# A hybrid attention and Fourier kernel: in its second mixer the products with the values follow the scores by two units instead of three, and query tiles are loaded one unit earlier

## The chip, the cores and the metric

The kernel runs on one core of a Trainium2 chip. The metric is device time in microseconds (us) of one execution, and lower is better. Three executions of the kernel before took 1214.49, 1209.16 and 1210.06 us, with a median of 1210.06 us. All times below the whole come from one more execution, the profiled one, which took 1214.27 us.

Engines are named as in the profile: PE is TensorE with PEld as its loading of weights, DVE is VectorE, ACT is ScalarE, POOL is GpSimd, and SP is the engine that issues the DMAs.

## The reference, cut to what matters

A step of a diffusion backbone has two layers over 1024 latent tokens and 256 context tokens, 1280 rows of 1024 channels. The even layer has two attention mixers: A is global, B looks at a window of 128 tokens on either side and at the context, with a learned "sink" logit per head. Each has 8 query heads and 2 key heads of 64 channels. The gated outputs of both are concatenated and projected. The odd layer is a Fourier mixer.

```python
oa = dense_block_attention(qa, ka ++ ka_ctx, va ++ va_ctx)      # mixer A: 1280 keys
ob = window_attention_with_ctx(qb, kb, vb, kb_ctx, vb_ctx, sink) # mixer B: up to 384 + 256 keys
y  = concatenate([oa * silu(ga), ob * silu(gb)], axis=-1) @ w_out
x  = x + gate * y
# odd layer
u, gate = split(h @ w_in);  y = (real(fft2(u)) * silu(gate)) @ w_out
```

All of it is float32. The kernel splits a float32 number into a high and a low part and forms a product as three matmuls, high by high, high by low and low by high (`mm3`, L256, whose matmuls have line L263).

## The kernel before

**Units.** The 1280 rows are 10 blocks of 128 rows. A unit of attention, written t_gp below, is a block t, a group g of four query heads (g 0 and 1 belong to mixer A, 2 and 3 to mixer B) and a pair p of those heads. So 6_30 is block 6, group 3, first pair. `attend` (L1077) goes through all 40 units of mixer A, and then through the 40 of mixer B in the order of blocks 0, 2, 3, 4, 7, 6, 5, 1, 8, 9 (`ORD_B`, L27), in which group 3 of a block comes four tiles behind its group 2.

**What a unit does.** `soft` (L932) forms the scores on PE (sL and sC at L924, in mixer B sC at L924 and the band sB at L996). DVE moves them out of PSUM and keeps the extreme of each row (`keep`, L958; in mixer B the mask at L1002). ACT then takes the exponential (L965) into a buffer of zone "p". `weigh` (L1031) transposes this buffer on PE, up to four squares to a PSUM bank (L1041), and ACT and DVE split each bank into a high and a low half of one buffer of zone "pt" (L275 and L1044). PE multiplies these by the values (tile av, L1047), and the result goes out to DRAM (tensor od, stored at L1064). Behind the second pair of group 3 `totals` (L1012) transposes the sums of the exponentials (tile tt, L1023) and stores them (tensor scd, L1028).

**The lag.** `attend` appends each unit's scores to a list, and runs `weigh` for the oldest while the list is longer than the lag: 1 unit in mixer A (`LAG_A`), 3 in mixer B (`LAG_B`). Zone "p" has 4 buffers. In mixer B a unit holds one of them.

**Query tiles.** The queries of a block and group are projected, transposed and split in `q_pair`, and written to DRAM (tensor qd). The tile that receives the split, qe, takes the zone in `QE_Z` ("pt", "q", "w", "u", "p") whose free buffer has been free for the longest. `load_q` (L926) reads a tile back by two DMAs of 64 partitions into one of the two buffers of zone "q". `attend` calls it for the next block and group behind the scores of a unit whose pair equals `QPRE` (L1087), which was 1, the second pair.

**Filler.** After each unit PE gets other work from a queue (`Filler`, L90): the projections of queries, keys and gates (ga, stored as tensor gd at L833 to L835), pieces that fold two weight matrices into one (wa, L557), and at the end the output projections. A step r of these is one block of 128 rows in the order 0, 4, 2, 6, 3, 7, 1, 5, 8, 9 (`PAIRS`, L61). Its load, `proj_in` (L1206), reads od, gd and scd, multiplies gate by sums (L1216) and that by od (L1217), and splits the result by ACT (L275) and DVE or POOL (L281). Its `proj_step` (L1315) runs 24 matmuls for each half of the columns, tiles oz{r}0 and oz{r}1 (so oz31 is the second half of step 3), and DVE scales each half (L1238) and adds it (L1239). A load is put into the queue ahead of the step before it.

**Buffers and order.** ZONES (L23) lists the buffers: 26 of "u", 8 of "w", 2 of "q", 3 of "pt", 4 of "p". Step 7's split lies in a "pt" and a "p" buffer, which become free only as the last units end. The program order above is input to a list scheduler (the tile context, L1947), which decides the order on each engine. Each engine then runs its own list in order, so that an instruction that waits holds up all behind it.

Of the kernel before, what the change touches and what calls it, by code (L numbers as in the profile page):

```python
# [22 lines left out]
ZONES = {"u": (26, 1032), "w": (8, 1032), "q": (2, 1024), "pt": (3, 1024), "p": (4, 1280), "h": (9, 512), "e": (4, 256)}  # L23
BIG = ("w", "q", "pt", "p", "u")
UV = ("u",)
FILL_A, FILL_B, LAG_A, LAG_B = 4.4, 2.9, 1, 3
E_PH, E_OH, E_OL, E_WO = "a", "a", "dp", "a"  # L27
EARLY, SPAN = 1, 2
WSTEP = ((2, 1, 2), (1, 0, 1))
# [9 lines left out]
E_ML = ("dp", "dp", "d")  # L39
E_MF, E_MH, LC0 = "da", "d", "ppd"  # L40
EF = 2
QPRE, HOLD = 1, 0
PLACE = (
    ((0, 0, 128),), ((128, 0, 128),), ((385, 0, 127), (256, 127, 1)), ((257, 0, 128),), ((769, 1, 127), (512, 0, 1)),
    ((896, 0, 128),), ((641, 0, 128),), ((513, 0, 128),), ((1024, 0, 128),), ((1153, 0, 127), (1152, 127, 1)),
# [94 lines left out]
def hybrid_step(ctx: ExitStack, tc: tile.TileContext, I, O):  # L140
# [15 lines left out]
    def take(tag, shape, dt=F32):  # L156
        tags = (tag,) if isinstance(tag, str) else tag
        z = min((t for t in tags if spare[t]), key=lambda t: spare[t][0])
        i = spare[z].popleft()[1]
        size = 2 if dt == BF16 else 4  # L160
        for s in shape[1:]:
            size *= s
        assert size <= 4 * ZONES[z][1]
        made[0] += 1
        return Buf(z, i, up.tile(list(shape), dt, tag=f"{z}{i}", name=f"{z}{made[0]}", bufs=1))
# [118 lines left out]
    def load_w(src, width=256, tags="w", gap=None, lc=E_WL, each=None, later=None):  # L284
        out = []
        for kp in range(2):
            hi = take(tags, (P, 4, width), F32R)
            lo = take(tags, (P, 4, width), F32R)
            for j in range(2):
                r0 = (kp * 4 + j * 2) * P  # L290
                if width <= 256:
                    raw = take("h", (P, 2, width))
                else:
                    raw = take(("p", "pt", "q", "w"), (P, 2, width))
                if gap is None:
                    sp.dma_start(raw.a, src[r0 : r0 + 2 * P, :].rearrange("(j p) f -> p j f", p=P))
                else:
                    gap(raw, r0)
                if each is not None:
                    each(raw, kp * 4 + 2 * j)  # L300

                def fin(raw=raw, hi=hi[:, 2 * j : 2 * j + 2, :], lo=lo[:, 2 * j : 2 * j + 2, :]):
                    split(hi, lo, raw.a, XE["wh"], lc)
                    drop(raw)

                if later is None:
                    fin()
                else:
                    later.append(fin)
            out.append((hi, lo))  # L310
        return out
# [239 lines left out]
    def fold_piece(g, kb2, wu, first=False):  # L551
        f = fold["f"]
        acc = bank("t" if first else "g", f"wa{g}{kb2}")
        for i in range(2):
            c0 = (2 * kb2 + i) * P
            for j in range(2):
                pe.matmul(  # L557
                    acc[:, i * 256 : i * 256 + 256], wu[j][:, c0 : c0 + P], f[:, j, :], start=j == 0, stop=j == 1
                )
        if first:  # L560
            if kb2 % 2 == 0:
                early[g, kb2 // 2] = take("u", (P, 4, 256))
            wo = early[g, kb2 // 2][:, 2 * (kb2 % 2) : 2 * (kb2 % 2) + 2, :]
        else:
            wb = take("h", (P, 2, 256))
            wo = wb.a
        copy("wo", "a", wo, acc.rearrange("p (i f) -> p i f", i=2))
        if not first:
            fold_put(g, kb2 * 256, wo)
            drop(wb)  # L570
        if kb2 == 3:
            drop(*wu)
            fold["n"] = fold.get("n", 0) + 1
            if fold["n"] in (EF, 4):
                drop(f)
                del fold["f"]
# [263 lines left out]
    fl_ = Filler()  # L840
# [343 lines left out]
    OB, late = [("u", "w")], [False]  # L1184
# [21 lines left out]
    def proj_in(src, gate, r, resid):  # L1206
        if gate is not None:
            flush_held()
            ol = take(OB[0], (P, 8, P))
            sp.dma_start(ol.a, src[r])  # L1210
            gl = take(OB[0], (P, 8, P))
            rl = take(OB[0], (P, 8, P))
            sp.dma_start(gl.a, gate[r])
            for h in range(2):
                sp.dma_start(rl[64 * h : 64 * h + 64], scd[r, h].partition_broadcast(64))
            pick("pm", XE["pm"]).tensor_mul(gl.a, gl.a, rl.a)  # L1216
            pick("pm", XE["pm"]).tensor_mul(ol.a, ol.a, gl.a)  # L1217
            drop(gl, rl)
        hi, lo = take(OB[0], (P, 8, P), F32R), take(OB[0], (P, 8, P), F32R)
        if gate is not None:  # L1220
            split(hi.a, lo.a, ol.a, E_OH, E_OL)
            drop(ol)
        else:
            for c in range(2):
                split(hi[:, 4 * c : 4 * c + 4, :], lo[:, 4 * c : 4 * c + 4, :], src(c, r), "a", "d")
        xr = take(OB[0], (P, D))
        sp.dma_start(xr.a, resid[r * P : (r + 1) * P, :])
        return hi, lo, xr
# [77 lines left out]
    def proj_load(i, j):  # L1306
        r = pairs[i][j]
        v = r // 8
        if v not in gt0:
            gt0[v] = take(OB[0], (P, D))  # L1310
            sp.dma_start(gt0[v].a, gtd[0, v].partition_broadcast(P))
        ins[r] = proj_in(od, gd, r, I["xp"])
        return 0
# [65 lines left out]
    def can_run(i, j):  # L1379
        r = pairs[i][j]  # L1380

        def fn():
            if sum(len(spare[z]) for z in OB[0]) < NSP or i > EARLY:
                return False
            return all(finished.get(t, 99) + SPAN < clock[0] for t in USES[r])
        return fn

    wgs = []
    steps = [(i, j) for i in range(5) for j in range(2)]

    def late_fold(nm):
        def fn():
            ws[nm] = fold_load(int(nm[1]))
            return 0
        return fn

    for n, nm in enumerate(FLATE.split()):
        fl_.add(0.0, late_fold(nm))
        if n == 0:
            fl_.add(0.0, lambda: proj_load(0, 0), ready=can_run(0, 0))  # L1400
        for k in range(4):
            fl_.add(FC, lambda k=k, nm=nm: fold_piece(int(nm[1]), k, ws[nm]))
    if not FLATE:
        fl_.add(0.0, lambda: proj_load(0, 0), ready=can_run(0, 0))
    for n, ij in enumerate(steps):
        if n == 8:
            fl_.add(0.0, lambda: wgs.append(load_w(I["w_g1"][:, 0:256], tags=BIG)) or 0)
        if n < 9:
            fl_.add(0.0, lambda ij=steps[n + 1]: proj_load(*ij), ready=can_run(*steps[n + 1]))
        fl_.add(7.7, lambda ij=ij: proj_step(*ij))  # L1410

    units = [(t, g, pr) for g in range(2) for t in range(NT) for pr in range(2)]
# [542 lines left out]
```

## Time and profile before

| What | Value |
|---|---|
| median of three runs | 1210.06 us (1209.16 to 1214.49) |
| profiled execution, its own time | 1214.27 us |
| span of its instructions | 1212.4 us |
| granted clock of TensorE, mean over the span | 0.985 of full speed |
| mixer A's units | about 137 to 520 us |
| mixer B's units | about 520 to 820 us |

The page gives busy time by engine and 40 slices of the span, each 30.3 us wide, in which a digit is the busy share in tenths. The time outside the span is 1.9 us. Where PE is idle, the views of waits and of the timeline tell what it waited for, and the view of windows gives busy time, granted clock and DMA share of any stretch.

### The profile page before, as it was taken

How to read it: one execution, taken by the hardware profiler on the slowest of the kernel's cores; microseconds unless marked ns; L12 is line 12 of the kernel's file. 1: busy time of each engine (PE TensorE's matmuls, PEld its weight loads, DVE VectorE, ACT ScalarE, POOL GpSimd, SP SyncE). 2: the span in 40 equal slices, each digit the busy share in tenths (PEclk: the TensorE clock that was granted, in tenths of full speed). 3: DMA queues.
4: the chain of work that ended last, by engine and by line, in shares of the span. 5: the costliest groups of instructions: out<-in, count | busy, mean ns of one | idle time of the engine just before them, and what ended most of it. 6: DMA issues, size and time to landing. Idle time of an engine off the chain costs nothing. (4 is left out here: it accounts for less than half of the span.)

```text
span 1212.4 us, 22083 instructions
## 1 busy us (share of the span) xinstructions
PE 1166.8 (96%) x8103; PEld 1041.6 (86%) x8103; DVE 839.6 (69%) x2000; ACT 576.6 (48%) x1159; POOL 320.1 (26%) x278
## 2 busy tenths in 40 slices
PE   7999999999999999999999999989999999999997
PEld 5787899999999998999888887868877888997886
DVE  3479788877777777678787776878756953367543
ACT  3343466555655555556566675533364224342211
POOL 2255634512332130011010114213202217245001
PEclk9899999999999999999999999989999999999999
DMA  9957412323523233344253686677214435264321
GB/s 317 360 190 260 150 59 66 103 79 108 149 64 101 60 92 113 95 120 121 74 140 81 181 256 198 181 201 219 96 44 136 152 114 169 94 200 151 121 103 53
DMA packets 129840, 168.81 MB, mean 139 GB/s; under 512 B 26298, under 2 KB 86454, under 8 KB 129732
## 3 DMA queue, kind: packets, MB, share of 16 engines
q1 hardware_dynamic: 129732, 167.40, 45.5%
q8 instruction: 64, 1.05, 0.4%
q14 instruction: 44, 0.36, 0.1%
HBM read 123.19 MB, written 44.16 MB: 138 GB/s over the span
## 5 line engine op out<-in xcount | busy, mean ns | idle before, releaser
L1044 DVE TENSOR_TENSOR pt<-pt,pt 128x512 fp32r<-128x512 f32 (+1 forms) x264 | 170.8, 658 | 50.9 <-ACT pt L275 50.1
L275 ACT ACTIVATE pt<-pt 128x512 fp32r<-128x512 f32 (+1 forms) x264 | 146.1, 575 | 83.9 <-PE pt L1041 49.0
L1047 PE MATMUL av<-pt,u 128*128 128x256 f32 x1008 | 167.3, 290 | 1.1 <-DVE e L1058 1.0
L1041 PE MATMUL pt<-identr,p 128*128 128x128 f32 x1008 | 153.7, 273 | 1.5 <-DVE pt L1044 1.5
L1047 PEld LDWEIGHTS av<-pt,u 128*128 128x128 f32 x1008 | 140.1, 190 | 6.2 <-DVE e L1058 2.0
L263 PE MATMUL q<-w,u 128*128 128x256 f32 x960 | 143.4, 287 | 0.2 <-ACT h L725 0.2
L263 PEld LDWEIGHTS q<-w,u 128*128 128x128 f32 x960 | 126.0, 189 | 5.1 <-issue 0.8
L1041 PEld LDWEIGHTS pt<-identr,p 128*128 128x128 f32 x1008 | 118.7, 141 | 7.0 <-issue 1.8
L263 PE MATMUL ga<-u,w 128*128 128x512 f32 (+1 forms) x576 | 124.2, 360 | 0.3 <-DVE h L817 0.2
L965 ACT ACTIVATE p<-p,nm 128x1280 f32<-128x1280 f32 (+1 forms) x80 | 95.3, 1192 | 53.4 <-DVE p L958 52.9
L263 PEld LDWEIGHTS ga<-u,w 128*128 128x128 f32 x576 | 93.6, 188 | 15.1 <-ACT pt L275 0.4
L281 POOL TENSOR_TENSOR w<-h,w 128x512 fp32r<-128x512 f32 x38 | 50.1, 1334 | 130.9 <-DVE w L277 100.4
L924 PE MATMUL sL<-u,q 128*128 128x512 f32 x256 | 82.4, 409 | 1.6 <-DMA q<-qd 1.6
L281 POOL TENSOR_TENSOR u<-h,u 128x512 fp32r<-128x512 f32 x24 | 33.8, 1416 | 158.7 <-ACT u L275 151.8
L965 ACT ACTIVATE p<-p,NM 128x640 f32<-128x640 f32 (+2 forms) x80 | 59.1, 739 | 24.5 <-DVE p L958 24.3
L924 PE MATMUL sC<-u,q 128*128 128x256 f32 x320 | 63.4, 297 | 4.0 <-DVE p L1002 2.0
L263 PE MATMUL oz<-u,u 128*128 128x512 f32 x208 | 60.8, 397 | 2.9 <-DVE h L1238 2.9
L263 PE MATMUL oz<-u,w 128*128 128x512 f32 x192 | 58.3, 396 | 0.0
L958 DVE TENSOR_SCALAR_CACHE_REDUCE p<-sL 128x512 f32<-128x512 f32 x64 | 43.8, 685 | 20.1 <-PE sL L924 15.3
L924 PEld LDWEIGHTS sC<-u,q 128*128 128x128 f32 x320 | 49.5, 190 | 7.7 <-DVE p L1002 2.6
L698 POOL TENSOR_TENSOR h<-h,rope 128x512 f32<-128x512 f32 (+1 forms) x18 | 21.2, 1180 | 128.2 <-ACT h L781 82.3
L958 DVE TENSOR_SCALAR_CACHE_REDUCE p<-sL,nm 128x512 f32<-128x512 f32 x64 | 47.6, 744 | 8.3 <-PE sL L924 7.0
(721 smaller groups left out, 2584.3 us busy)
## 6 DMA issues: line engine op xcount, KB each, us to landing
q<-qd SPq DMA_DIRECT2D x80, 256.0 KB
h<-i_w_in SPq DMA_DIRECT2D x40, 256.0 KB
p<-i_ada_w SPq DMA_DIRECT2D x18, 512.0 KB
qd<-q SPq DMA_DIRECT2D x36, 256.0 KB
h<-i_w_out SPq DMA_DIRECT2D x32, 256.0 KB
pt<-i_ada_w SPq DMA_DIRECT2D x15, 512.0 KB
q<-i_ada_w SPq DMA_DIRECT2D x11, 512.0 KB
u<-g1d SPq DMA_DIRECT2D x9, 512.0 KB
```

Source lines behind the costliest of these rows:

```text
L263: pe.matmul(out, a, b, start=i == 0, stop=i == n - 1)
L275: act.activation(out, in_, AF.Copy)
L281: pick("lo" + lc, lc).tensor_sub(dst_l, src, dst_h)
L698: pick("rope", XE["rope"]).tensor_mul(t1.rearrange("p t h (b c) -> p t (h b) c", b=2), y.rearrange("p t h (b c) -> p t (h b) c", b=2), cb)
L924: pe.matmul(ps, q_at(q, s, hc), keys, start=s == 0, stop=s == 1)
L958: dve.tensor_scalar(p[i][:, end[i] : end[i] + n], ps, sign, last[i], op0=ALU.mult, op1=ALU.min, accum_out=c)
L965: act.activation(p[i][:, 0 : end[i]], p[i][:, 0 : end[i]], AF.Exp, bias=last[i], scale=-1.0, accum_out=SU[:, t, hd + i, 0:1],)
L1041: pe.transpose(tp[:, jj * 256 + i * P : jj * 256 + i * P + P], p[i][:, off : off + P], ident)
L1044: dve.tensor_sub(pt[:, 1, 0:n], tp[:, 0:n], pt[:, 0, 0:n])
L1047: pe.matmul(acc, vv, pt[:, s, jj * 256 : jj * 256 + 256], start=c + jj + s == 0, stop=c + jj == nt - 1 and s == 1,)
```

## The change

`LAG_B` becomes 2. `QPRE` becomes 0: the next query tile is loaded behind the first pair of a tile, not the second, in both mixers. The loads of the projections go through `load_to`, which with `AHEAD` at 1 issues the same load at the same place as before.

```diff
-FILL_A, FILL_B, LAG_A, LAG_B = 4.4, 2.9, 1, 3
+FILL_A, FILL_B, LAG_A, LAG_B = 4.4, 2.9, 1, 2
-QPRE, HOLD = 1, 0
+QPRE, HOLD, AHEAD = 0, 0, 1
...
+    loaded = [0]
+
+    def load_to(n):
+        while loaded[0] <= min(n, 9):
+            proj_load(*steps[loaded[0]])
+            loaded[0] += 1
+        return 0
...
-            fl_.add(0.0, lambda: proj_load(0, 0), ready=can_run(0, 0))
+            fl_.add(0.0, lambda: load_to(0), ready=can_run(0, 0))
...
-            fl_.add(0.0, lambda ij=steps[n + 1]: proj_load(*ij), ready=can_run(*steps[n + 1]))
+            fl_.add(0.0, lambda n=n: load_to(n + (AHEAD if late[0] else 1)), ready=can_run(*steps[n + 1]))
```

Since the scheduler orders the whole program, rows move on every engine. Three places are shown. In a row the numbers behind a name are the program's own and differ between the two kernels.

On SP, around the query tile of block 6, group 3, before. The first and the last row are the two halves of the tile (q926); between them stand stores of attention outputs (od), of sums (scd) and of gates (gd), two loads of step 0 (u919, u920) and a store of fold work (wd); the line of dots leaves out two stores of od and one of scd.

```order
L929 DMA q926_9263<-qd_69 64x2x512
...
L1028 DMA scd_77<-e882_8972 16x1
L833 DMA gd_73<-h909_9203 128x128
L834 DMA gd_73<-h909_9203 128x127
L835 DMA gd_73<-h909_9203 128x1
L1213 DMA u919_9230<-gd_73 128x1024
L1064 DMA od_72<-e881_8959 64x2x127
L1064 DMA od_72<-e881_8959 64x2x1
L1215 DMA u920_9231<-scd_77 64x1024 x2
L547 DMA wd_74<-h924_9248 128x2x256
L929 DMA q926_9263<-qd_69 64x2x512
```

The same place now; the tile is q908.

```order
L929 DMA q908_9176<-qd_69 64x2x512
L1064 DMA od_72<-e858_8781 64x2x127
L1064 DMA od_72<-e858_8781 64x2x1
L1028 DMA scd_77<-e875_8907 16x127
L1028 DMA scd_77<-e875_8907 16x1
L833 DMA gd_73<-h890_9045 128x128
L834 DMA gd_73<-h890_9045 128x127
L835 DMA gd_73<-h890_9045 128x1
L1064 DMA od_72<-e874_8894 64x2x127
L1064 DMA od_72<-e874_8894 64x2x1
L929 DMA q908_9176<-qd_69 64x2x512
```

The second half stands 10 rows behind the first, not 13, and the loads of step 0 (u919, u920) and the store wd are no longer ahead of it.

On PE, between the second pair's scores of block 6, group 3 and the first transposes of its first pair (pt6_300), before.

```order
L996 MATMUL sB6_310_9416<-u682_7065,q926_9263 128x384 x2
L996 MATMUL sB6_311_9421<-u682_7065,q926_9263 128x384 x2
L924 MATMUL sC6_31_9409<-u684_7067,q926_9263 128x256 x2
L1041 MATMUL pt8_210_9480<-identr_85,p925_9253 128x128 x4
L1047 MATMUL av7_31_9347<-pt937_9353,u684_7067 128x256 x4
L1047 MATMUL av7_31_9347<-pt938_9365,u683_7066 128x256 x4
L557 MATMUL wa31_9398<-h914_9219,w934_9319 128x256
L557 MATMUL wa31_9398<-h914_9219,w935_9320 128x256
L557 MATMUL wa31_9398<-h914_9219,w934_9319 128x256
L557 MATMUL wa31_9398<-h914_9219,w935_9320 128x256
L1041 MATMUL pt6_300_9513<-identr_85,p936_9325 128x128
```

Now, with the last score row of 6_30 as the first row here.

```order
L924 MATMUL sC6_30_9371<-u683_7045,q908_9176 128x256 x2
L924 MATMUL sC6_31_9431<-u683_7045,q908_9176 128x256 x2
L1041 MATMUL pt8_200_9396<-identr_85,p907_9166 128x128 x4
...
L996 MATMUL sB6_310_9438<-u681_7043,q908_9176 128x384 x2
L996 MATMUL sB6_311_9443<-u681_7043,q908_9176 128x384 x2
L924 MATMUL sC6_31_9431<-u683_7045,q908_9176 128x256 x2
L1041 MATMUL pt8_210_9452<-identr_85,p930_9287 128x128 x4
L1047 MATMUL av7_31_9297<-pt931_9303,u683_7045 128x256 x4
L1047 MATMUL av7_31_9297<-pt932_9315,u682_7044 128x256 x4
L1041 MATMUL pt6_300_9501<-identr_85,p941_9370 128x128
```

The fold piece that stood right ahead of pt6_300 is gone from there (four rows of another piece, wa21, stand in the place of the line of dots), and so are the value products of 7_30 and the transposed sums tt7, which before stood between the last sC6_30 and the scores of 6_31.

On PE, the end of mixer B, before: the last rows of the second half of step 3, the value products of 9_30, and the start of step 7.

```order
L1047 MATMUL av8_31_10228<-pt1039_10234,u684_7067 128x256 x4
L1023 MATMUL tt9_10306<-identr_85,byp9_10304 16x128
L263 MATMUL oz61_10355<-u911_9210,u1008_9955 128x512
L263 MATMUL oz61_10355<-u910_9209,u1009_9956 128x512
L263 MATMUL oz31_10463<-u816_8428,w1053_10321 128x512
...
L263 MATMUL oz31_10463<-u910_9209,u1054_10322 128x512
L1047 MATMUL av9_30_10260<-pt1043_10266,u684_7067 128x256 x4
L263 MATMUL oz70_10509<-u816_8428,pt1066_10427 128x512
```

Now.

```order
L1047 MATMUL av8_31_10229<-pt1039_10235,u683_7045 128x256 x4
L263 MATMUL oz31_10463<-u822_8470,w1053_10321 128x512
L263 MATMUL oz31_10463<-u823_8471,w1053_10321 128x512
L1023 MATMUL tt9_10306<-identr_85,byp9_10304 16x128
...
L263 MATMUL oz60_10327<-u916_9243,u1014_10006 128x512
L263 MATMUL oz60_10327<-u915_9242,u1015_10007 128x512
L263 MATMUL oz31_10463<-u916_9243,w1053_10321 128x512
L263 MATMUL oz31_10463<-u915_9242,u1054_10322 128x512
L1047 MATMUL av9_31_10279<-pt1046_10285,u683_7045 128x256 x4
L263 MATMUL oz71_10537<-u822_8470,pt1066_10427 128x512
```

Between av8_31 and the first matmul of step 7 stand 48 matmuls of L263 and the value products of 9_30 and 9_31, where before 26 matmuls and the value products of 9_30 stood. The second half of step 3 runs ahead of the first half of step 6, and step 7's second half ahead of its first.

In mixer A the query evictions of `q_pair` move too: of the 20 tiles qe, 18 lay in zone "q", one in "pt" and one in "p"; now 9 lie in "q", 10 in "pt" (among them qT004, qT008, qT112 and qT116) and one in "p".

More of the change, by code (lines that the diff above doesn't have):

```diff
@@ L1403, in hybrid_step @@
     if not FLATE:
-        fl_.add(0.0, lambda: proj_load(0, 0), ready=can_run(0, 0))
+        fl_.add(0.0, lambda: load_to(0), ready=can_run(0, 0))
     for n, ij in enumerate(steps):
```

## The prediction

> **What bounds the kernel.** I read the page first, then windows, then PE's waits.
>
> ```profile
> span 1212.4 us, 22083 instructions
> PE 1166.8 (96%) x8103; PEld 1041.6 (86%) x8103; DVE 839.6 (69%) x2000; ACT 576.6 (48%) x1159; POOL 320.1 (26%) x278
> PE   7999999999999999999999999989999999999997
> PEclk9899999999999999999999999989999999999999
> ```
>
> PE is busy for 1166.8 of 1212.4 us, so only 45.6 us of its idle time can be won at all, plus what a lowered clock costs. The change touches mixer A (about 137 to 520 us) in one place and mixer B (520 to 820) everywhere. The one slice with an 8 in the middle of PE's row, the 27th, is 788 to 818 us, the end of mixer B, and the clock row has its 8 there too.
>
> ```profile
> 200.00:500.00 300.00, 298.37 (x2296) 284.49 (x2294) 225.93 (x543) 171.96 (x307) 75.31 (x71) 1.00 0.33 94
> 600.00:700.00 100.00, 94.69 (x615) 84.85 (x614) 77.13 (x236) 62.12 (x142) 10.31 (x8) 0.98 0.48 134
> 700.00:800.00 100.00, 95.15 (x560) 84.00 (x559) 71.04 (x201) 56.53 (x136) 27.79 (x13) 0.98 0.74 210
> 800.00:850.00 50.00, 44.92 (x186) 35.94 (x185) 41.42 (x53) 14.55 (x21) 13.54 (x7) 0.90 0.67 205
> 850.00:900.00 50.00, 50.00 (x247) 41.01 (x246) 34.57 (x54) 23.59 (x43) 8.33 (x7) 1.00 0.19 71
> 618.00:626.00 8.00, 5.10 (x25) 4.52 (x24) 6.35 (x18) 6.71 (x17) 2.05 (x2) 0.79 0.55 157
> 709.00:716.00 7.00, 5.14 (x22) 4.60 (x22) 3.95 (x10) 3.25 (x6) 4.70 (x2) 0.76 1.05 327
> 812.00:822.00 10.00, 8.98 (x26) 6.86 (x27) 8.90 (x16) 2.64 (x4) 2.97 (x2) 0.60 0.60 150
> ```
>
> The columns are the stretch, its length, the busy time of PE, PEld, DVE, ACT and POOL, the granted clock of PE, the DMA share and GB/s. Mixer A's 300 us leave PE 1.6 us idle. From 600 to 850 us it is idle 5.3 + 4.9 + 5.1 = 15.2 us, and not at all in the next 50. The last three rows hold the lowered clocks of this part: (1 − 0.79) × 8 = 1.7 us, (1 − 0.76) × 7 = 1.7 us and (1 − 0.60) × 10 = 4.0 us of PE work were lost there. PE's waits from 500 to 850 us (in total, times, longest):
>
> ```profile
> PE oz L263 <- ACT pt L275: 4.1, 1, 4.1
> PE oz L263 <- DVE h L1238: 2.9, 1, 2.9
> PE sC L924 <- DVE p L1002: 2.0, 1, 2.0
> PE sC L924 <- DMA q<-qd: 2.0, 1, 2.0
> PE pt L1041 <- DVE pt L1044: 1.5, 4, 0.8
> PE av L1047 <- DVE e L1058: 1.0, 1, 1.0
> ```
>
> A few single waits bound this part, not a steady one: two at output projections (oz), two at scores (sC). So the change is worth what it does to each.
>
> **The change part by part.** It adds and removes no arithmetic: PE keeps its work, and what moves is when each wait is met. `load_to` issues the same loads as before, so it is worth 0.
>
> *Query tile (the wait of 2.0).*
>
> ```profile
> 694.38 0.60 SPq L929 DMA_DIRECT2D q<-qd  x1
> 705.22 0.60 SPq L929 DMA_DIRECT2D q<-qd  x1
> 710.86 0.77 PE L924 MATMUL sC<-u,q 128*128 128x256 f32 x2 [1.97 <-DMA q<-qd]
> ```
>
> The two halves of the tile of block 6, group 3 were issued 10.8 us apart, since SP stood before stores and loads in between, and PE went on 5.6 us after the second. Now SP has 10 rows from one half to the other, not 13, step 0's loads stand behind them, and the tile's load comes one unit earlier. By the PE work between, 8 to 10 us more lie ahead of its scores, against 1.97 us needed. The wait goes, and with it the clock lost beside it: 1.97 + 0.24 × 7 = 3.65 us. Bounds: 0 (SP waits as long elsewhere) and −3.6. I take **−3.6**.
>
> [...]
>
> *End of mixer B (the waits of 4.1 and 1.0).*
>
> ```profile
> 800.67 0.63 PE L1047 MATMUL av<-pt,u 128*128 128x256 f32 x4
> 801.33 0.32 SPq L1213 DMA_DIRECT2D pt<-gd  x1
> 801.71 0.63 PE L263 MATMUL oz<-u,w 128*128 128x512 f32 x2
> 806.93 0.67 DVE L1238 TENSOR_TENSOR h<-oz,u 128x512 f32<-128x512 f32 x1
> 810.87 1.06 ACT L275 ACTIVATE pt<-p 128x1024 fp32r<-128x1024 f32 x1 [1.08 <-DVE p L1217]
> 811.97 2.08 PE L263 MATMUL oz<-u,pt 128*128 128x512 f32 x4 [4.06 <-ACT pt L275]
> ```
>
> Step 7 loads its gate into a "pt" buffer which the last products of unit 8_31 (800.67) give up. From the load (801.33) to the end of the split (810.87 + 1.06 = 811.9) its chain takes 10.6 us, and PE had 26 matmuls and four value products for it, 7.2 us. Now it has 48 matmuls of L263 and eight value products. By the row of 24 below (5.80 / 24 = 0.24 each) the 22 more are 5.3 us, so 12.5 us against 10.6 plus what little lies ahead of the load: the wait of 4.06 is gone, and the 1.02 behind it, and the 4.0 us of clock from 812 to 822 with them: −9.1.
>
> What is late next are the other steps, whose order changed:
>
> ```profile
> 741.88 5.80 PE L263 MATMUL oz<-u,w 128*128 128x512 f32 x24
> 834.06 3.43 POOL L281 TENSOR_TENSOR w<-u,w 128x1024 fp32r<-128x1024 f32 x1 [16.11 <-ACT w L275]
> 844.61 3.63 PE L263 MATMUL oz<-u,w 128*128 128x512 f32 x15
> 792.66 1.23 DVE L281 TENSOR_TENSOR u<-w,w 128x1024 fp32r<-128x1024 f32 x1 [0.64 <-ACT w L275]
> ```
>
> Step 3's split ended at 792.66 + 1.23 = 793.9 us and its first matmul came at 801.71, so it had 7.8 us to spare. From step 4's end to it stood 96 matmuls, now 72: 24 fewer, 5.8 us. One more product (L1216, 1.2 us as such products of 128x1024 take here) now precedes it on DVE. 0.8 us are left: no wait, by little. Step 5's split waits for buffers that step 6's end gives up: from there (its last matmuls end at about 801.9, beside step 3's first) to the split's end (834.06 + 3.43 = 837.5) went 35.6 us, and its first matmuls stand in the row of 844.61. Now only some 29 us of PE work lie between. The shortfall is 6.6 us if the chain takes as long as before; but 5 us of it were lost at its start (801.9 to 806.93, DVE standing behind step 7's DMA), and these need not recur. Bounds: 0 to 6.6; I take 3 back, half-way, as neither row is nearer. Sum of the end: **−6**.
>
> *Wait of 2.9 at step 0.*
>
> ```profile
> 751.05 1.23 DVE L281 TENSOR_TENSOR w<-w,u 128x1024 fp32r<-128x1024 f32 x1 [6.71 <-ACT u L275]
> 752.93 0.73 PE L263 MATMUL oz<-u,u 128*128 128x512 f32 x2 [2.88 <-DVE h L1238]
> ```
>
> PE waits for the bank that DVE should empty (L1238); DVE stands 6.71 us at a split of step 2, whose gates come from folds that end about 730 us. The PE work from those folds to step 4 is 19.8 us before and 19.0 now, so nothing frees DVE earlier in any way that I see. Bounds: −2.9 (DVE's order changes) and +0.8 (the shorter distance); I take **0**, nearest to the kept distance.
>
> *The two score waits on DVE (L1002) and pt (L1044), around 620 and 694 us.* They follow landings of output weights, on which ACT stands, and the change does not touch these loads, though their place may shift. Bounds: ±5, a wait like the one at 618 to 626 (2.9 idle and 1.7 of clock) gained or doubled. I take **0**.
>
> *The shorter lag.* A unit's first transposes now come one unit earlier after its scores, and must not overtake its exponential.
>
> ```profile
> 715.60 0.48 PE L924 MATMUL sC<-u,q 128*128 128x256 f32 x2
> 720.20 0.82 ACT L965 ACTIVATE p<-p,NM 128x640 f32<-128x640 f32 x1
> 721.66 1.89 PE L557 MATMUL wa<-h,w 128*128 128x256 f32 x8
> 723.39 0.93 PE L1041 MATMUL pt<-identr,p 128*128 128x128 f32 x7
> ```
>
> In unit 6_30 the last score ended at 716.1 us, its exponential at 721.0, 4.9 us later, and its transposes began at 723.39. The fold ahead of them (1.89 us) is gone from there, the products of 7_30 and tt7 too, and another fold stands there, so that by the PE work between some 4.8 us are left (four of the fold's rows, 1.89, and eight transposes, six score rows and eight value products), against 4.9: 0.1 us of waiting. The next tightest units have 6.0 and 6.9 us. Bounds: 0 and +4 (the exponential late by a us or so in four units); I take **0**. The "p" ring is easier now, since three units and not four hold buffers; a gain of PE's from that has no wait to come from.
>
> *Mixer A's ring.* Nine more query evictions take one of three "pt" buffers.
>
> ```profile
> L275 ACT ACTIVATE pt<-pt 128x512 fp32r<-128x512 f32 x126 | 71.5, 595 | 49.0 <-PE pt L1041 29.6 <-PE av L1047 12.8 <-DVE p L958 4.2
> ACT pt L275 <- PE av L1047: 16.0, 15, 2.1
> ```
>
> In 300 us 126 transposed tiles pass: one each 2.4 us, a turn of the ring each 7.1. A query tile holds its buffer for its copy and subtraction (0.6 and 0.7) and its two stores, about 1.2 to issue and the 5.6 that a query DMA took above to land: 8.1, 1.0 more than a turn. ACT already waits for the ring 15 times, 1.1 us on average and 2.1 at most (second row), and PE is idle 1.6 us all the same, so the filler hides such waits. Cost if that cover is gone: 9 × 1.1 = 9.6 to 9 × 2.1 = 18.9 us. Bounds: 0 to 18.9; I take **0**, by PE's idle 1.6 us.
>
> *Sum.* −3.6 − 6 − 0 = −9.6 us, on 1214.27 us 1204.7. The profiled execution lies 4.2 us above the median of the runs; taken off 1210.06, the sum gives 1200.5. I cannot tell which of its waits the faster runs lack, so I forecast the middle, **1202.5 us**. A measurement of this kernel tells some 0.5% from no change: below 1204.0 is faster, above 1216.1 slower.
>
> **The rivals.**
>
> *Only the query wait goes* (0.24). The end of mixer B trades step 7's wait for one at step 5 or 3: 0.8 us of slack at step 3 and a shortfall of up to 6.6 at step 5 speak for it, the 5 us lost at the start of step 5's chain against it. 1210.06 − 3.6 = 1206.4, with 1204 to 1212.
>
> *Everything goes* (0.08). All 15.2 us idle and 1.7 + 1.7 + 4.0 us of clock: 1210.06 − 22 = 1188, up to 1192 if something stays. DVE's untouched queue at 751 speaks against it.
>
> *Mixer A's ring decides* (0.19). If the query tiles' stores hold "pt" for longer than a turn plus what filler covers, ACT falls behind, PE's transposes wait for their banks and the units slip: 1202.5 + 18.9 = 1221, between 1217 and 1230. It decides from the point where a query store keeps its buffer over 7.1 us and the wait exceeds the 2.1 us that ACT is seen to bear. For it speaks the 8.1 above; against it a DMA share of 0.33 in mixer A where the 5.6 was measured at 1.05.
>
> *The change does not do what it says* (0.04): the scheduler restores the old distances, 1210. The orders of PE and SP speak against it.
>
> **How the numbers follow.** The forecast has 0.45, with a range of its own of 1198 to 1207: 0.34 below 1204.0 and 0.11 above. Faster is 0.34 + 0.08 = 0.42, within 0.5% is 0.11 + 0.24 + 0.04 = 0.39, slower 0.19. The range goes from 1192, which leaves out "everything goes", to 1219, which leaves out the upper half of the ring's case: some 0.08 + 0.11 left out.
>
> **What would show it.** Right: no PE wait for a query DMA near 710; no wait of an oz matmul for ACT (L275) near 810; clock 1.00 where it was 0.60. Wrong: PE waits for DVE (L1044 or L958) at transposes in mixer B (lag); a wait at step 5 or 3 of over 3 us between 800 and 850 (end); PE idle in 200 to 500 well above 1.6 us, with ACT's wait for the ring above 16 us (mixer A); ACT or DVE at output weights near 620 and 694 longer than now. The prediction fails most easily in the scheduler's new order of DVE, which I priced only at steps 0, 3 and 5.

## The result and the profile after

The changed kernel took 1201.3 us in the median (1200.58 to 1202.03, four runs), against 1209.87 for the kernel before (1209.16 to 1214.49, four runs). The ratio is 0.9921 with a 95% interval of 0.9895 to 0.9947. The forecast was 1202.5, 1.2 us above. As the rest shows, only some of the steps to it were right.

The page of the changed kernel, and its windows (same columns as before):

```profile
span 1200.2 us, 22028 instructions
PE 1162.1 (97%) x8103; PEld 1038.7 (87%) x8103; DVE 831.7 (69%) x2000; ACT 578.5 (48%) x1159; POOL 319.1 (27%) x278
PE   7899899999999999999999979999999999999997
PEclk9899999999999999999999989999999999999999
```

```profile
200.00:500.00 300.00, 299.74 (x2316) 286.15 (x2315) 224.08 (x549) 174.10 (x308) 77.66 (x73) 1.00 0.33 93
600.00:700.00 100.00, 98.37 (x658) 88.96 (x657) 83.50 (x258) 67.46 (x156) 10.35 (x8) 1.00 0.50 136
700.00:800.00 100.00, 93.06 (x523) 80.70 (x522) 70.19 (x186) 51.45 (x122) 28.15 (x13) 0.97 0.74 223
800.00:850.00 50.00, 50.00 (x220) 40.55 (x219) 38.62 (x54) 17.39 (x24) 15.53 (x9) 1.00 0.67 217
618.00:626.00 8.00, 7.22 (x47) 6.26 (x47) 6.95 (x19) 7.21 (x16) 1.30 (x1) 1.00 0.71 196
710.00:720.00 10.00, 3.79 (x11) 3.28 (x12) 3.84 (x10) 4.31 (x10) 3.82 (x2) 0.67 0.73 214
812.00:822.00 10.00, 10.00 (x45) 8.10 (x44) 9.31 (x9) 1.93 (x2) 0.00 (x0) 1.00 0.81 248
```

The span is 12.2 us shorter (1212.4 − 1200.2). The stretch 600 to 700 won 3.7 us of idle time, 800 to 850 won 5.1 and has its full clock, but 700 to 800 lost 2.1: PE's row has a new 7 there, in the 24th slice (690 to 720 us), the clock row has its 8 in that slice, and from 710 to 720 PE works for 3.79 of 10 us at a mean clock of 0.67. PE's waits from 500 to 850 us say what stands behind it:

```profile
PE sC L924 <- DMA q<-qd: 6.6, 1, 6.6
PE sB L996 <- DVE p L1002: 0.5, 1, 0.5
PE ga L263 <- DVE h L817: 0.3, 1, 0.3
```

All the waits of the kernel before are gone but for rests of half a microsecond. A query wait, which the prediction took away, is the only large one left, now 6.6 us. SP's and PE's timelines around it:

```profile
683.00 0.59 SPq L929 DMA_DIRECT2D q<-qd  x1
690.66 0.60 SPq L929 DMA_DIRECT2D q<-qd  x1
...
704.33 1.36 SPq L542 DMA_DIRECT2D w<-i_wuT  x2
707.72 0.60 SPq L929 DMA_DIRECT2D q<-qd  x1
709.57 0.59 SPq L929 DMA_DIRECT2D q<-qd  x1
```

```profile
716.21 1.19 PE L924 MATMUL sC<-u,q 128*128 128x256 f32 x4 [6.59 <-DMA q<-qd]
```

The first two rows are the tile of block 6, group 3, on which the kernel before waited. It was issued by 690.66 and its scores began at 696.5, without a wait. The last two are the tile behind it, block 9, group 2. Its buffer was free when the scores of unit 8_21 ended, at 696.3 us, but SP came to it 11 us later. In between SP issued the five loads of output step 0 (694 to 703 us) and a fold's weights (wuT, 1 MB), and stood for landings of these loads, as SP's waits from 690 to 720 us show:

```profile
SPq L929 <- DMA u<-gd: 2.0, 1, 2.0
SPq L547 <- DMA w<-i_wuT: 1.5, 1, 1.5
SPq L1064 <- DMA u<-gtd: 1.3, 1, 1.3
```

At the end of mixer B, the chain of step 7 and that of step 5:

```profile
792.61 0.32 SPq L1213 DMA_DIRECT2D pt<-gd  x1
799.89 1.05 ACT L275 ACTIVATE pt<-q 128x1024 fp32r<-128x1024 f32 x1
804.97 0.62 PE L263 MATMUL oz<-u,pt 128*128 128x512 f32 x2
825.14 2.41 POOL L281 TENSOR_TENSOR w<-u,w 128x1024 fp32r<-128x1024 f32 x1 [17.53 <-ACT w L275]
832.61 1.56 PE L263 MATMUL oz<-u,w 128*128 128x512 f32 x6
```

Step 7's high part is ready at 800.9 us, 4 us before PE needs it. Step 5's split ends at 827.6, 5 us before its first matmuls: from step 6's last matmul (its end at 804.2) to there it took 23.4 us, where before it took 35.6.

### The profile page after: what moved, and what is told of

Its sections match the earlier page's. It is cut to its first block, busy times and chain, and to the rows that moved or that the text cites. A ratio compares the mean times of both kernels' runs of the same rounds, so it can differ in the third digit from the quotient of the medians.

```text
span 1200.2 us, 22028 instructions
## 1 busy us (share of the span) xinstructions
PE 1162.1 (97%) x8103; PEld 1038.7 (87%) x8103; DVE 831.7 (69%) x2000; ACT 578.5 (48%) x1159; POOL 319.1 (27%) x278
## 3 DMA queue, kind: packets, MB, share of 16 engines
q8 instruction: 64, 1.05, 0.4%
## 5 line engine op out<-in xcount | busy, mean ns | idle before, releaser
L1047 PE MATMUL av<-pt,u 128*128 128x256 f32 x1008 | 165.6, 287 | 0.1
L1041 PE MATMUL pt<-identr,p 128*128 128x128 f32 x1008 | 154.6, 272 | 0.4 <-DVE pt L1044 0.3
L263 PE MATMUL q<-w,u 128*128 128x256 f32 x960 | 144.5, 288 | 0.2 <-ACT h L725 0.2
L1047 PEld LDWEIGHTS av<-pt,u 128*128 128x128 f32 x1008 | 138.1, 189 | 3.7 <-DVE pt L1044 0.8
L263 PEld LDWEIGHTS q<-w,u 128*128 128x128 f32 x960 | 127.5, 190 | 5.9 <-issue 0.8
L1041 PEld LDWEIGHTS pt<-identr,p 128*128 128x128 f32 x1008 | 118.9, 140 | 7.0 <-PE sB L996 0.9
L263 PE MATMUL ga<-u,w 128*128 128x512 f32 (+1 forms) x576 | 124.5, 360 | 0.3 <-DVE h L817 0.3
L263 PEld LDWEIGHTS ga<-u,w 128*128 128x128 f32 x576 | 93.9, 188 | 14.5 <-ACT e L1056 0.5
L263 PE MATMUL oz<-u,u 128*128 128x512 f32 x208 | 59.6, 396 | 0.1
L263 PE MATMUL oz<-u,w 128*128 128x512 f32 x192 | 58.2, 395 | 0.0
```

The costliest lines, as they stand in the source:

```text
L263: pe.matmul(out, a, b, start=i == 0, stop=i == n - 1)
L1041: pe.transpose(tp[:, jj * 256 + i * P : jj * 256 + i * P + P], p[i][:, off : off + P], ident)
L1047: pe.matmul(acc, vv, pt[:, s, jj * 256 : jj * 256 + 256], start=c + jj + s == 0, stop=c + jj == nt - 1 and s == 1,)
```

## The experiments

Each kernel is the changed one but for the edit shown. "Before" was timed again beside each group; its medians there were 1212.0 to 1212.6 us, against 1209.9 beside the changed kernel, so ratios are the safer comparison, and a difference between two experiments of less than some 3 us is not read. The waits named are those of one profiled execution each. Some of these were faster than the median: 1197.6 us with both edits (median 1203.6), 1204.3 with a lag of one (1208.2), 1207.0 with 1 MB more (1209.9).

| Kernel | median, us (range) | ratio to before (95%) |
|---|---|---|
| changed | 1201.3 (1200.6 to 1202.0) | 0.9921 (0.9895 to 0.9947) |
| lag alone | 1201.6 (1200.5 to 1202.5) | 0.9907 (0.9894 to 0.992) |
| query loads alone | 1210.7 (1205.2 to 1214.8) | 0.9987 (0.9973 to 1.0002) |
| no pt for query evictions | 1204.4 (1202.3 to 1206.0) | 0.993 (0.9917 to 0.9942) |
| one tile by POOL's queue | 1206.7 (1205.3 to 1208.4) | 0.9952 (0.994 to 0.9964) |
| row of gates early | 1201.0 (1198.7 to 1207.1) | 0.9913 (0.989 to 0.9935) |
| fold's weights early | 1207.1 (1204.5 to 1210.0) | 0.9955 (0.9937 to 0.9973) |
| 1 MB more loads | 1209.9 (1206.7 to 1213.4) | 0.9976 (0.996 to 0.9992) |
| a p buffer parked | 1205.6 (1204.4 to 1208.3) | 0.9944 (0.9928 to 0.9959) |
| tile ahead of the fold's weights | 1206.7 (1202.8 to 1210.9) | 0.9958 (0.9939 to 0.9977) |
| the same, and gates early | 1203.6 (1197.6 to 1208.2) | 0.9926 (0.9898 to 0.9954) |
| lag of one | 1208.2 (1204.3 to 1213.2) | 0.9968 (0.9953 to 0.9983) |
| lag of two only late | 1212.1 (1208.3 to 1217.7) | 0.9995 (0.9977 to 1.0013) |

**The two parts of the change apart.**

```diff
-QPRE, HOLD, AHEAD = 0, 0, 1
+QPRE, HOLD, AHEAD = 1, 0, 1
```

> The changed kernel with the query tiles loaded as before (QPRE 1), so the lag alone. Theory A (as in the prediction: the earlier load is worth its own 3.6 us, the lag is worth the end of mixer B): the waits at step 7 (4.1 us), step 0 (2.9) and at the scores near 620 and 694 stay away, but the time is some 4 us above the changed kernel, about 1205 us. Theory B (the trace of the changed kernel shows a wait of 6.6 us for the tile of block 9, group 2, behind a burst of loads on SP, and this burst stands in the same place with either setting): the lag makes the whole gain and the earlier load none; 1199 to 1203 us, with a wait of 5 to 8 us for a query DMA near 710.

```diff
-FILL_A, FILL_B, LAG_A, LAG_B = 4.4, 2.9, 1, 2
+FILL_A, FILL_B, LAG_A, LAG_B = 4.4, 2.9, 1, 3
```

> The kernel before with the query tiles loaded one unit earlier (LAG_B 3, QPRE 0). Theory A: 1206 us, the wait of 2.0 us for a query DMA gone and the rest as before. Theory B: the load only shifts which tile meets the burst of loads; 1208 to 1213 us, a query wait of 2 us or more stays somewhere in 690 to 730, and so do waits of 3 us and more at the output projections (oz).

The lag alone gives 1201.6 us, the whole gain. Its waits on PE from 500 to 860 us begin with

```profile
PE sC L924 <- DMA q<-qd: 4.8, 2, 4.6
```

so the query wait is there with the loads as late as before (4.6 us at 713.48, where 5 to 8 were expected). The query loads alone give 1210.7 us, no measurable gain, and scatter from 1205 to 1215. Their profiled execution, one of the faster ones (1206.55), still has single waits, at other places and smaller than theory B asked for:

```profile
710.78 2.00 PE L557 MATMUL wa<-h,w 128*128 128x256 f32 x8 [2.15 <-ACT h L275]
721.31 0.47 PE L924 MATMUL sC<-u,q 128*128 128x256 f32 x2 [1.22 <-DMA q<-qd]
806.99 1.22 PE L263 MATMUL oz<-u,w 128*128 128x512 f32 x2 [1.98 <-DVE e L1058]
```

Theory B held in the times: the lag makes the gain, and loading queries one unit earlier makes none that can be measured, with either lag.

That does not mean that the earlier load does nothing. From the first value product of mixer A (L1047) to the first band scores of mixer B (L996) the profiles show 381.9 us before and 382.1 with the lag alone, and 378.9 to 380.1 in the twelve kernels that load queries one unit earlier. So mixer A is some 2 to 3 us shorter with it. In the changed kernel this is lost again behind it: from 500 to 850 us PE is idle for 8.6 us, and for 6.2 with the lag alone.

**Mixer A's ring.**

```diff
-QE_Z = ("pt", "q", "w", "u", "p")
+QE_Z = ("q", "w", "u", "p")
```

> The changed kernel, but the query evictions of mixer A may not take a pt buffer (pt left out of QE_Z). The prediction's rival that the ring in mixer A costs time: the time falls by 3 us or more below the changed kernel's 1201.3. My forecast (no cost): the same within 2 us, and PE idle in 200 to 500 us unchanged at about 0.3 us.

PE is idle for 0.02 us in 200 to 500 (0.26 in the changed kernel, 1.63 before), and the time is 1204.4, not lower: above the 2 us that I allowed, but by its ratio (0.993 against 0.9921) the same. The rival that query evictions in "pt" cost time in mixer A falls.

**What holds the tile of block 9.** Five kernels move or add transfers around 695 us, where the loads of step 0, the fold's weights and the query tiles meet.

```diff
-            sp.dma_start(q[64 * i : 64 * i + 64], qd[t, g].rearrange("(h d) f -> d h f", d=64))
+            eng = nc.gpsimd if (t, g) == (9, 2) else sp
+            eng.dma_start(q[64 * i : 64 * i + 64], qd[t, g].rearrange("(h d) f -> d h f", d=64))
```

> The changed kernel, with the one tile of block 9, group 2 loaded by POOL's queue and not SP's. Theory B1 (the tile is late because SP, which issues in order, stands behind the landings of other loads; its buffer was free at 696.3 us and SP came to it at 707.7): the wait of 6.6 us goes and the clock lost beside it, about 3 us; 1192 to 1195 us. Theory B2 (the DMA engines are full, so the tile lands as late whichever queue issues it): the wait stays above 4 us and the time within 3 us of 1201.3. Theory B3: the time is won there and lost later at steps 0, 4 or 2, whose loads come as late: 1197 to 1201 us with new waits at oz between 730 and 790.

```diff
+    def gate_row():
+        gt0[0] = take("p", (P, D))
+        sp.dma_start(gt0[0].a, gtd[0, 0].partition_broadcast(P))
+        return 0
...
+        if gi == 2:
+            fl_.add(0.0, gate_row)
```

> The changed kernel, but the 512 KB row of gates (gtd) of the first output projection step is loaded into a p buffer, about 30 us ahead of the burst of loads near 695 us, not within it. Theory C (the burst is bound by DMA bandwidth: some 4.5 MB at about 280 GB/s between the end of the last gate work and the tile of block 9, group 2): 0.5 MB less is 1.9 us less of the wait of 6.6 us, and some clock; 1196 to 1199 us. Theory D (the gain of the changed kernel came from the p ring, in which a lag of 2 leaves one buffer spare, here taken by the gates): the waits on DVE near 620 us do not change, as the gates come later, but those behind 670 us come back; 1203 us or more.

```diff
-        if n == 0:
+        if n == 1:
             fl_.add(0.0, lambda: load_to(0), ready=can_run(0, 0))
```

> The changed kernel, but the first output projection step's loads are put into the queue behind the last fold's load (1 MB of wuT), so that this 1 MB goes ahead of the tile of block 6, group 3 and not into the burst. Theory C: the wait at the tile of block 9, group 2 falls by 1 MB / 280 GB/s = 3.7 us to about 3, unless the tile of block 6 meets the 1 MB; 1194 to 1198 us. Rival (DMA work is only shifted to another tile): a query wait of 3 us or more near 695 and the time within 2 us of 1201.3.

```diff
         ins[r] = proj_in(od, gd, r, I["xp"])
+        if r == 0:
+            more = [take(OB[0], (P, D)) for k in range(2)]
+            for k in range(2):
+                sp.dma_start(more[k].a, I["xp"][k * P : (k + 1) * P, :])
+            drop(*more)
```

> The changed kernel with 1 MB of further loads (two blocks of the input, into two buffers that nothing reads) in the first output projection step's load. Theory C: the wait for the tile of block 9, group 2, grows by 0.5 to 1 MB at 280 GB/s, 1.9 to 3.7 us, to 8.5 to 10.3 us (or this much in it and in the fold behind it together), and the time to 1203.5 to 1206. Rival (the wait is set by SP's order and by when buffers come free, not by bandwidth): the wait stays at 6 to 7 us and the time within 1.5 us of 1201.3.

```diff
-        q = take("q", (P, 2, 512))
+        q = take("w" if (t, g) == (9, 2) else "q", (P, 2, 512))
...
+            if un == (8, 2, 1):
+                qs[(9, 2)] = load_q(9, 2)
```

> The changed kernel with the tile of block 9, group 2 in a w buffer, its load put one unit earlier: on SP it now stands ahead of the last fold's 1 MB, not behind, and the tile of block 5, group 3 follows it. If this 1 MB is what holds the tile (1 MB / 280 GB/s = 3.7 us), the wait of 6.6 us falls to 3 or less and the time to 1194 to 1198 us, unless the fold then waits for its weights. If the stretch from 690 to 730 us is bound by its DMA bytes as a whole (PE's idle time there was 6.0 to 6.8 us in five kernels with the loads in different orders), the idle time there stays above 5 us and the time within 3 us of 1201.3.

The last one is this and the row of gates together.

> The same with the row of gates loaded some 30 us early as well, so 1.5 MB less ahead of the tile of block 9, group 2. If single loads ahead of a tile decide, its wait is gone and the time 1193 to 1197 us. If the bytes of the stretch as a whole decide, 0.5 MB fewer gives 1 to 2 us: 1199 to 1201. The p buffer that the gates hold costs what the parked buffer cost behind 670 us (of 4.3 us in all): up to 2 us more.

With the tile on POOL's queue, POOL issues it at 698.75 us, 9 us before SP had. PE then waits 0.67 us for it, but the next tile (block 5, group 3) comes late instead:

```profile
698.75 1.42 POOL L930 DMA_DIRECT2D q<-qd  x2
```

```profile
709.73 0.48 PE L924 MATMUL sC<-u,q 128*128 128x256 f32 x2 [0.67 <-DMA q<-qd]
719.64 0.61 PE L924 MATMUL sC<-u,q 128*128 128x256 f32 x2 [3.07 <-DMA q<-qd]
```

The issue (B1) was one part of it: from the end of the issue (700.2) PE's scores still came only at 709.7, 9.5 us later, beside a DMA share of 1.05 from 700 to 710 us. The other kernels read alike. With the gates early the wait at block 9 is gone, and 3.50 us stand at block 5's tile, 1.33 at block 6's, and 1.54 at an exponential. With the fold's weights early, 2.10, 0.78 and 1.94 us stand at three tiles. With the tile ahead of the weights, 2.10 us stand at block 9's and 3.56 at block 5's:

```profile
712.16 0.47 PE L924 MATMUL sC<-u,w 128*128 128x256 f32 x2 [2.10 <-DMA w<-qd]
718.02 0.47 PE L924 MATMUL sC<-u,q 128*128 128x256 f32 x2 [3.56 <-DMA q<-qd]
```

The row from 690 to 730 us of six of these kernels: the changed one, the lag alone, POOL's queue, the gates early, the tile ahead, and both.

```profile
690.00:730.00 40.00, 33.20 (x219) 30.79 (x219) 25.70 (x78) 24.64 (x60) 8.73 (x5) 0.91 0.87 248
```

```profile
690.00:730.00 40.00, 35.16 (x225) 32.53 (x224) 27.93 (x78) 24.07 (x59) 10.77 (x5) 0.91 0.91 255
```

```profile
690.00:730.00 40.00, 32.74 (x201) 29.13 (x200) 26.46 (x77) 22.97 (x58) 10.89 (x7) 0.91 0.88 240
```

```profile
690.00:730.00 40.00, 33.63 (x206) 30.68 (x206) 27.84 (x81) 25.01 (x60) 13.10 (x6) 0.91 0.82 243
```

```profile
690.00:730.00 40.00, 33.78 (x224) 31.16 (x223) 24.05 (x76) 24.36 (x61) 9.40 (x5) 0.96 0.85 237
```

```profile
690.00:730.00 40.00, 33.61 (x225) 30.64 (x224) 27.85 (x85) 27.14 (x67) 13.12 (x6) 1.00 0.90 251
```

PE is idle 4.8 to 7.3 us in each, at a DMA share of 0.82 to 0.91, however the loads are ordered. So in these kernels the wait belongs to the stretch, not to one tile: the transfer that is helped passes its delay to the next. That bytes alone bind the stretch is not settled. With a lag of 3 up to there PE is idle less in the same stretch: 3.6 us before (DMA share 0.81), 3.5 with the query loads alone (0.85), 4.9 with the late lag (0.79). With 1 MB more the time rose by 8.6 us (some 6.7 by the ratios), more than the 2 to 5 of the forecast, but its wait for the tile was 5.77 us and not the 8.5 to 10.3 expected, and the rest appeared in other places (1.31 us at a query tile at 759, 1.66 at step 3 at 794, 2.13 at 811). With 0.5 MB taken out ahead of the stretch the time stayed (1201.0). The last of the kernels has the shortest span of all in its profiled execution, 1195.8 us, but its runs go from 1197.6 to 1208.2, and its interval does not part it from the changed kernel. POOL's queue, the fold early and the tile ahead came out slower than any of their theories said, some 5 us above the changed kernel (ratios 0.995 to 0.996). From 500 to 850 us PE is idle 12.0, 10.7 and 12.2 us in them, against 8.6 in the changed kernel, and the surplus lies outside 690 to 730; what causes it was not tried. None of these kernels beats the lag alone.

**Where the rest of the gain comes from.**

```diff
+    parked = take("p", (P, 1280))
     attend([(t, g, pr) for t, g in seq for pr in range(2)], fill, LAG_B, after)
+    drop(parked)
```

> The changed kernel with one of the four p buffers taken out through mixer B, so that a unit's scores wait for the transposes of the unit three before, as tight a ring as before (lag + 1 buffers). Theory D (the waits near 620, 694 and 753 us went because the ring has a spare buffer at lag 2): DVE waits for transposes again (before: 3.3 us in 4 places), some of the waits of 2 to 3 us at scores come back and the time is 1204 to 1209. Theory E (they went because the order of ACT and DVE shifted against the landings of the output weights): within 1.5 us of 1201.3.

```diff
-FILL_A, FILL_B, LAG_A, LAG_B = 4.4, 2.9, 1, 2
+FILL_A, FILL_B, LAG_A, LAG_B = 4.4, 2.9, 1, 1
```

> The changed kernel with LAG_B 1. By PE's order the least distance from a unit's last scores to its first transposes hardly shrinks, as the scheduler spaces them itself, and step 7's first half starts 5 us of PE work earlier. If the ring's spare buffers give the gain, a second spare gives little more (before: 3.3 us of waits for it, 0 in the changed kernel), and the time stays within 3 us of 1201.3; if the distance to the exponentials decides, PE waits for ACT (L965) at transposes in several units and the time is 1204 or more.

```diff
-            while len(pend) > lag:
+            while len(pend) > (3 if lag > 1 and n < 32 else lag):
```

> The changed kernel with a lag of 3 for the first 32 units of mixer B and of 2 for the last 8 (from block 5, group 3 on). The prediction's account of the end (a lag of 2 puts more work between unit 8_31 and step 7) needs the lag of 2 only in the last units: no wait for ACT's split at step 7, and with a score wait of 2 us at 620 and some query wait kept some 4 to 6 us above the changed kernel, 1203 to 1207 us. Rival (the gain is made before the last units: there the lag of 2 frees the ring and lets the filler run in another order, and the end follows from that): PE's order from 8_31 to step 7 stays near that of a lag of 3 (29 matmuls of L263 between, against 48), waits of 2 us and more at oz behind 790 us stay, and the time is 1208 to 1212, as with the query tiles alone (1210.7).

Who waited for transposes (L1041) from 500 to 850 us: DVE's row of the kernel before, and that of the kernel with a parked buffer. The changed kernel has no such row.

```profile
  DVE p L958: 3.3, 4
```

```profile
  DVE p L958: 5.5, 6
```

With it the score wait at 620 us is back, nearly in its old size (2.05 before):

```profile
619.06 0.50 PE L924 MATMUL sC<-u,q 128*128 128x256 f32 x2 [1.87 <-DVE p L1002]
```

The time is 1205.6 us, 4.3 above the changed kernel, or 0.9944 against 0.9921 and, with the lag alone, 0.9907. So some 30 to 50% of the gain needs the spare "p" buffer that a lag of 2 leaves; the interval is clear of the lag alone's, not of the changed kernel's. The size of the wait at 620 us is not set by the ring alone: with a lag of 3 and the queries early, a ring as tight, it is 0.89 us. A second spare gives nothing more: with a lag of 1 no DVE wait for transposes is left either, yet the time is 1208.2. Its waits are for query tiles (6.1 us in three places), and the clock from 690 to 730 us is 0.87. Waits for the exponential, the price I had looked for, are not among them.

A lag of 2 in the last 8 units alone gives 1212.1 us, nothing. Its waits at 620 us are the same as with the query loads alone (0.89 and 0.85), and the end of mixer B has one as large as before, though DVE (L1058) and not ACT's split releases it:

```profile
712.38 3.42 PE L557 MATMUL wa<-h,w 128*128 128x256 f32 x8 [3.90 <-ACT h L275]
812.47 1.22 PE L263 MATMUL oz<-u,w 128*128 128x512 f32 x2 [4.24 <-DVE e L1058]
```

So the lag of the last 8 units alone does not win the end; that of the 32 units ahead is needed too, I think through the order in which the scheduler then lays the output steps. That these 32 alone would do was not tried.

## Why the prediction was right or wrong

- **The sum was right, its terms were not.** Forecast −9.6 us on the profiled execution, measured −12.2 in span and −8.6 in the medians. In the terms of the prediction the profiles show: query tile +4.9 (forecast −3.6), end −8.7 (−6), step 0 −2.9 (0), the waits near 620 and 694 us −5.2 (0), all ahead of mixer B −0.8 (0; its first scores come 0.8 us earlier). That makes −12.7, close to the span's. The errors of the first and of the next three largely cancelled, and that is luck.
- **Query tile: wrong, and the step that failed is "the wait goes, and with it the clock lost beside it".** The working looked at one tile, block 6's, and that tile did come in time. It did not ask which tile is next to meet the loads of step 0 that "stand behind" it. That was block 9's: 6.59 us of wait and 2.0 us of clock, in place of 1.97 and 1.7. Apart, the two settings show that the earlier load is worth nothing in the end (1201.6 with the old one).
- **End of mixer B: the wait went as forecast (4.06, 1.02 and the clock), and nothing was given back.** Of the 4.0 us of clock 3.6 were PE's work; in the rest PE was idle. Of the two next-late steps, step 3 came without a wait, as worked out; step 5's chain fell from 35.6 to 23.4 us, by 12.2 and not the 5 that I allowed, so the 3 us back were too many. The reason that I gave stands half: the 48 matmuls are there and cover step 7's chain, but a lag of 2 in the last units does not bring it about, as the run with a late lag shows.
- **Step 0's wait: wrong by 2.9.** I kept it since the distance from the folds to step 4 hardly moved. It is 0 in the changed kernel and 0.45 in the one with the earlier queries alone. I had named a new order of DVE's as the bound, but that is not what the rows show. DVE still scales the second half of step 0 (L1238) behind step 2's split, at 752.19 behind 751.05 before, and now:

```profile
748.23 5.75 PE L263 MATMUL oz<-u,w 128*128 128x512 f32 x24
753.33 1.23 DVE L281 TENSOR_TENSOR w<-w,u 128x1024 fp32r<-128x1024 f32 x1 [1.10 <-ACT u L275]
755.27 0.69 DVE L1238 TENSOR_TENSOR h<-oz,u 128x512 f32<-128x512 f32 x1
```

  PE comes to that half 6.4 us later than before (748.23, 741.88), the split only 2.3 us later, so the bank is empty in time. PE is late there partly from its wait at the query tile, so some of that wait may be paid back here; no run parts the two.
- **Score waits near 620 and 694 us: wrong, and the step that failed is "a gain of PE's from that has no wait to come from".** They looked like waits for output weights, on which ACT and then DVE stood (before, ACT 2.03 us at 616.77 for a DMA of w_out, DVE 2.53 at 619.61 for ACT's split). The parked buffer shows that the ring of "p" was part of it: with it, 1.87 of the 2.05 us come back. The wait near 694 is at the transposed sums, in a row of PE's waits before that the prediction's list leaves out:

```profile
PE tt L1023 <- DVE pt L1044: 1.4, 1, 1.4
```

- **The shorter lag itself: right.** The tightest unit, 6_30, has its last exponential at 705.4 us and its transposes at 706.1. No PE wait for ACT's exponential is among the changed kernel's waits. It is tight, though: with the gates early it is 1.54 us.
- **Mixer A: right that the "pt" ring costs nothing, wrong by some 2.7 us in the gain.** Without the "pt" buffers nothing was won. But mixer A took 379.2 us and not 381.9; only 0.8 of it shows in the start of mixer B, since the changed kernel's execution came to mixer A 1.9 us later (148.6 us, before 146.7). PE's idle time from 200 to 500 us fell from 1.6 to 0.3. The earlier query loads bring this, as the kernels without them lack it.
- **The clock.** The wait of 6.59 us cost 2.0 us of clock, hardly more than the 1.7 of the one of 1.97 before. Taken in windows of 3.41 us, the rows show why (two of the kernel before, then three of the changed one; the third number from the end is the clock):

```profile
707.45:710.86 3.41, 1.45 (x14) 1.24 (x12) 1.05 (x3) 2.82 (x7) 1.53 (x1) 1.00 1.03 297
710.86:714.28 3.42, 3.42 (x10) 2.97 (x11) 2.62 (x7) 0.14 (x1) 3.17 (x2) 0.50 1.05 362
709.97:713.38 3.41, 0.00 (x0) 0.00 (x0) 0.00 (x0) 0.00 (x0) 3.33 (x2) 1.00 0.79 220
713.38:716.79 3.41, 0.58 (x3) 0.61 (x4) 1.32 (x2) 2.53 (x5) 0.52 (x1) 0.50 0.40 122
716.79:720.21 3.42, 3.42 (x11) 2.79 (x11) 2.52 (x8) 1.78 (x6) 0.00 (x0) 0.50 1.05 313
```

  The clock is 1.00 or 0.50 here, and values like 0.76 and 0.67 are means over a stretch. At half clock PE's work took longer: in the changed kernel eight fold matmuls (L557) took 3.38 us from 717.20 on and 1.89 at full clock from 722.04 on. I count half of PE's work in these rows as lost, an estimate: half of 3.42 us before, half of 0.58 + 3.42 now. The 2.83 us of the fourth row in which PE stood idle are not counted. The steps of 3.41 us are read from the profiles: in the kernel before half clock began at 622.12, 710.86 and 809.85 us, 26 and 29 times 3.41 us apart, and lasted 3.41, 3.41 and 10.24 us; in the changed kernel it began at 713.38 and lasted 6.83. The step ahead of it had 1.96 us of PE's idle time in the first row, and 3.41 in the third. The wait of 2.88 us at step 0 was followed by no half clock; counted on in such steps, it leaves PE idle for 1.78 us in one (748.41 to 751.83) and 1.10 in the next. That the place of a wait among these steps sets what it costs is my guess from these rows; no run moved a wait by itself.

## What to carry to other kernels

When a wait for a transfer goes because the transfer is issued earlier, look at the next transfer on the same queue and in the same stretch: here the burst of loads passed its delay on (1.97 us at block 6's tile before, 6.59 at block 9's now), and a forecast that follows one tile counts the gain and not its heir. A lag between producer and consumer also sets how many buffers of the ring are spare; before pricing such a wait at nothing, count the buffers before and after, and ask which engine in front of the ring holds others up. Where a scheduler lays out the order, test each part of a change apart, over the stretch and at its end, before saying which part made the gain.

## What the runs showed of the hardware

- A query tile of two halves, 256 KB each, let PE go on 5.0 us after the end of its second issue in the kernel before (705.82 to 710.86, DMA share 0.98 between them), and 9.5 us after it from POOL's queue (700.17 to 709.73, DMA share 1.05 from 700 to 710).
- SP stood at a DMA until earlier transfers had landed that this DMA does not read: by the changed kernel's profile, from 690 to 720 us, 2.0 us for the gates ahead of the query tile, 1.5 for the fold's weights ahead of a store, 1.3 for the gates' row ahead of another store.
- From 500 to 860 us TensorE was granted 1.00 or 0.50 of its clock in the profiles of the kernel before and the changed one. Half clock began at 622.12, 710.86 and 809.85 us and lasted 3.41, 3.41 and 10.24 us before; it began at 713.38 us and lasted 6.83 in the changed kernel. Taken in steps of 3.41 us from these starts, PE was idle for 2.84, 1.96 and 1.93 us in the steps ahead of half clock before, and for 3.41 in the changed kernel; of the steps that no half clock followed, the two with the most idle time had 1.78 and 1.10 us (both before, from 748.41 on). Within half clock, steps with 2.12 and 1.02 us of idle time (before) and 2.83 (changed) were followed by half clock again, those with 0.06 us or less by the full clock. Two profiles give no limit between these numbers.
- Runs of the same kernel scatter by as much as the variants differ: query loads alone from 1205.2 to 1214.8 us, both edits from 1197.6 to 1208.2, the changed kernel's four runs from 1200.6 to 1202.0. What differs between such runs was not found. A part lies ahead of mixer A, whose first value product began at 146.7 us in the profiled execution of the kernel before and at 148.6 in that of the changed one.
